# Channel-first inputs, norms on VectorE and combinations on GpSimd in a Strassen-like first stage

## The chip, the cores and the metric

One core of a Trainium2 chip runs one launch. The metric is the device time of that launch in microseconds (us). Engines: TensorE (PE; its weight loads are PEld), VectorE (DVE), ScalarE (ACT), GpSimd (POOL), and SyncE (SP), which issues most DMAs.

## The reference

A gated encoder layer is applied to two token sets, `x_prompt` (1024 tokens of 1024 channels) and `x_sample` (512 tokens). Cut to what matters:

```python
h = rms_norm(x, pre_w)                       # x * rsqrt(mean(x*x) + eps) * pre_w, per token
cols = jnp.einsum('bsd,dc->bsc', h, w_in)    # one combined projection for all branches
...                                          # mLSTM branch, dilated attention branch, gates
out = jnp.einsum('bsd,de->bse', merged, w_out)
return x + rms_norm(out, post_w)
```

Everything is float32, and the change lies in how `h` is made and laid out for the combined projection.

## The kernel before

A float32 product is made of three passes (`mm3`, L193 to L195): every operand is split into a high part, rounded to the format that PE takes at full rate (`AF.Copy` on ACT), and a low part, the difference (on DVE).

For the prompt, `h` (tokens by channels) is divided into four quarters of 512x512, and the projection is a seven-product scheme on 2x2 blocks (Strassen's, in Winograd's form). The seven combinations of quarters are B11, T2, B21, T3, T1, T4 and B22. Each is needed by channel (channels on the 128 partitions, tokens along the row), because PE sums over the partitions. They are kept in `H[0][m]` (high, `Hh`) and `H[1][m]` (low, `Hl`), each 128 x 4 x 512, `k` counting the four groups of 128 channels.

With x(i, j) the quarter of token block i and channel block j after the norm, T1 is x(1,0) - x(0,0), T3 is x(1,1) - x(1,0), T2 is x(1,1) - T1, T4 is x(0,1) - T2; B11, B21 and B22 are x(0,0), x(0,1) and x(1,1).

`value_group(g)` makes the value and gate columns for g = 0 to 3. Group 0 runs first, while the inputs arrive, in the order m1 (B11), m2 (B21), m7 (T3), m6 (T2), m5 (T1), m4 (T4), m3 (B22); each product is 48 matmuls of 128x322. Its weights `wa` and `wb` are summed on DVE (`sums`, and `s[:, 1]` once more after m6's split), and `split` makes high and low parts into two rotating pairs of buffers `vhi`, `vlo`.

The pieces around the change, before:

- `lead` (L344): per token block of 128, ACT squares a row tile and sums it, POOL makes the reciprocal root (`root`, L253), DVE puts it on a diagonal, and PE multiplies the raw rows by this diagonal, which transposes and scales them at once. That gives B11.
- `norm` (L356): DVE scales the whole rows, 128x1024, in place (L359, L266).
- `put(m, k)` (L368): PE transposes, with sums and differences where the combination needs them (products with the identity or its negative, L377 and L379), ACT makes the high part from the bank, and DVE the low part (L383), or, for B21 and B22, PE subtracts the high part in the bank (L387) and ACT copies the rest.
- These calls stand between the quarters of the products (`with_m1` to `with_m6`), so PE's order interleaves them with matmuls.
- `sub` (L361): DVE makes x(1,0) - x(0,0), and x(1,1) minus that, on rows.
- `short_input` (L719): the sample's rows, normed at the end of the first stage, are transposed by PE at the start of the second stage (`turn_in`, L268).

PE's order is the order of the code (`manual_schedule`). The other engines' orders in this first stage are fixed when the program is built, by a scheduler with its own estimates; each engine then runs its instructions strictly in that order, waiting where an input is missing.

Of the kernel before, what the change touches and what calls it, by code (L numbers as in the profile page):

```python
# [176 lines left out]
class Net:  # L177
# [90 lines left out]
    def turn_in(self, parts, ps, out, k, w=None):  # L268

        nc = self.nc  # L270
        p = ps.tile([P, BLK], F32, name="d")
        for t, x in enumerate(parts):
            nc.tensor.transpose(p[:, t * P:(t + 1) * P], x[:, k * P:(k + 1) * P], self.ident)
        hi, lo = (x[:, k] for x in out)
        if w is None:
            end = nc.scalar.activation(hi, p, AF.Copy)
            nc.vector.tensor_sub(lo, p, hi.bitcast(F32))
        else:
            end = nc.scalar.activation(hi, p, AF.Copy, scale=w)
            nc.vector.scalar_tensor_tensor(lo, p, w, hi.bitcast(F32), op0=OP.mult, op1=OP.subtract)  # L280
        return end
# [48 lines left out]
    def combos(self, ps, H, xt, r, junk, pw, minus, again, diag):  # L330

        nc = self.nc
        part = lambda i, j: [x[:, j * BLK:(j + 1) * BLK] for x in xt[i]]
        a0, b0, a1, b1 = part(0, 0), part(0, 1), part(1, 0), part(1, 1)
        plus, neg = self.ident, minus.bitcast(F32)  # L340
        terms = {B21: [(b0, plus)], B22: [(b1, plus)], T3: [(b1, plus), (a1, neg)],
                 T1: [(a0, plus)], T2: [(b1, plus)], T4: [(b0, plus), (b1, neg)]}

        def lead():  # L344
            ps_ = [ps.tile([P, BLK], F32, name="d") for _ in range(4)]
            for t in range(4):
                nc.vector.tensor_scalar(diag[t], self.ident, self.root(xt[0][t], r[t], junk), None, op0=OP.mult)
                for k in range(4):
                    nc.tensor.matmul(ps_[k][:, t * P:(t + 1) * P], a0[t][:, k * P:(k + 1) * P], diag[t], start=t == 0,
                                     stop=True, skip_group_check=True)  # L350
# [5 lines left out]
        def norm(i, t):  # L356
            if i:
                return self.norm(xt[i][t], r[4 * i + t], junk, pw)
            return nc.vector.scalar_tensor_tensor(xt[i][t], xt[i][t], r[t][:, 2:3], pw, op0=OP.mult, op1=OP.mult)  # L359

        def sub(m):  # L361
            for t in range(4):
                if m == T1:
                    nc.vector.tensor_sub(a0[t], a1[t], a0[t])
                else:
                    nc.vector.tensor_sub(b1[t], b1[t], a0[t])

        def put(m, k):  # L368

            if m == T4 and k == 0:  # L370
                again()
            p = ps.tile([P, BLK], F32, name="d")
            for t in range(4):
                for i, (x, one) in enumerate(terms[m]):
                    of, to = x[t][:, k * P:(k + 1) * P], p[:, t * P:(t + 1) * P]
                    if i == 0 and m not in (B21, B22):
                        nc.tensor.transpose(to, of, one)  # L377
                    else:
                        nc.tensor.matmul(to, of, one, start=t == i == 0, stop=True, skip_group_check=True)  # L379
            hi, lo = H[0][m][:, k], H[1][m][:, k]  # L380
            nc.scalar.activation(hi, p, AF.Copy)
            if m not in (B21, B22):
                self.low = nc.vector.tensor_sub(lo, p, hi.bitcast(F32))  # L383
                return None

            def rest():
                nc.tensor.matmul(p, minus, hi, start=False, stop=True, skip_group_check=True)  # L387
                nc.scalar.activation(lo, p, AF.Copy)
            return rest

        return lead, norm, sub, put
# [11 lines left out]
    def value_group(self, g, T, H, sb, us, co, ps, late=None, begin=None, u3=None, more=None, turn=None):  # L403
# [8 lines left out]
        if g:  # L412
            first, wa, wb, s = place(), *self.value_weights(sb)
            for kh in range(2):
                nc.sync.dma_start(wa[:, kh], self.a["w_vp"][g, 0, kh])
            for kh in range(2):
                nc.sync.dma_start(wb[:, kh], self.a["w_vp"][g, 1, kh])
        else:
            first, wa, wb, s, (lead, norm, sub, put) = begin
# [11 lines left out]
        def product(m, w, turns=(), outer=False):  # L431

            banks = [ps.tile([P, BLK], F32, name="d") for _ in range(4)]
            turns = iter(turns)
            if outer:
                next(turns)
            for i in range(4):
# [5 lines left out]
                next(turns, None)  # L443
# [26 lines left out]
        if g == 0:  # L470
            lead()
            w11, low = split(wa[:, 0], first, 2), []

            def with_m1():
                yield
                with self.tc.issue_after(self.low.ins):
                    for t in range(4):
                        last = norm(0, t)
                yield
                with self.tc.issue_after(last.ins):  # L480
                    for t in range(4):
                        last = norm(1, t)
                yield
                low.append(last.ins)
                rest = [put(B21, 0)]
                yield
                for k in range(1, 4):
                    rest.append(put(B21, k))
                    rest.pop(0)()
                rest.pop(0)()  # L490
                yield

            def with_m2():
                rest = [put(B22, 0), put(B22, 1)]
                yield
                rest += [put(B22, 2), put(B22, 3)]
                rest.pop(0)(), rest.pop(0)()
                yield
                put(T3, 0)
                rest.pop(0)(), rest.pop(0)()  # L500
                put(T3, 1)
                yield
                put(T3, 2), put(T3, 3)
                low.append(self.low.ins)
                yield

            def with_m7():
                put(T1, 0), put(T1, 1)
                yield
                put(T1, 2), put(T1, 3)  # L510
                with self.tc.issue_after(low[1]):
                    sub(T2)
                yield
                put(T2, 0), put(T2, 1)
                yield
                put(T2, 2), put(T2, 3)
                low.append(self.low.ins)
                yield

            def with_m6():  # L520
                for k in range(4):
                    put(T4, k)
                    yield

            m1 = product(B11, w11, with_m1(), True)
# [3 lines left out]
            with self.tc.issue_after(low[0]):  # L529
                self.sums(wa, wb, s)  # L530
            m2 = product(B21, w12, with_m2())
# [4 lines left out]
            with self.tc.issue_after(low[0]):  # L536
                sub(T1)
# [3 lines left out]
            with self.tc.issue_after(low[1]):  # L541
                s2 = split(s[:, 1])
            m6 = product(T2, s2, with_m6())
            with self.tc.issue_after(low[2]):
                nc.vector.tensor_sub(s[:, 1], wa[:, 1], s[:, 1])
            for t in range(4):
                add(u2[t], u2[t], m6[t][:, :VW])
                add(u3[t], u3[t], m6[t][:, :VW])
            yield
# [27 lines left out]
        if g == 0:  # L577
            with self.tc.issue_after(low[2]):
                s1 = split(s[:, 0])
        else:  # L580
            s1 = split(s[:, 0])
        m5 = product(T1, s1)
        if g == 0:
            for t, c in enumerate(held):
# [9 lines left out]
        m4 = product(T4, split(wb[:, 1]))  # L594
        for t in range(4):
# [123 lines left out]
    def short_input(self, ps, xt):  # L719
# [1113 lines left out]
def body(tc, a):  # L1833
# [3 lines left out]
    with ExitStack() as st:  # L1837
# [12 lines left out]
        with ExitStack() as s1:  # L1850
# [4 lines left out]
            with ExitStack() as sv:  # L1855
# [5 lines left out]
                one = us.tile([P, VW], F32, name="u2", bufs=4)[0:1, :P]  # L1861
                diag = [us.tile([P, VW], F32, name="u2b", bufs=4)[:, :P] for _ in range(4)]
                xp = N.pool(s3, "x0", 1, "left"), N.pool(s4, "x1", 1, "right")
                xt = [[xp[i].tile([P, D], F32, name=f"x{i}{t}") for t in range(4)] for i in range(2)]
                minus = H[1][T4][:, 3, :P]
                spare = H[0][T4].bitcast(F32).rearrange("p a c -> p (a c)")
# [250 lines left out]
```

## Time and profile before

| | |
|---|---|
| median of 3 runs | 2289.6 us (2284.14 to 2295.39) |
| profiled execution | 2292.12 us, span 2290.3 us |
| PE busy | 2258.5 us, 99% of the span |
| DVE, ACT, POOL busy | 1465.7, 1102.2, 628.6 us |
| first product of group 0 starts | 13.49 us |
| second stage's first product starts | 978.07 us |

A row of a timeline has start, length, engine, line, operation, `output<-inputs`, shapes, count, and in brackets the idle time of the engine before it and what ended it. A row of a group has the count, then busy time and the mean in ns. A row of busy time by stretches has the stretch, its length, busy time of PE, PEld, DVE, ACT and POOL with their counts, the granted clock, the DMA engines' share and GB/s. Names leave out buffer numbers: `Hh`, `Hl` are the combinations, `x` the input tiles.

### The profile page before, as it was taken

Reading aid. Unit: us, or ns where it says so; the run is one execution under the profiler, and the core shown is the slowest. Engines: PE = TensorE matmul, PEld = TensorE weight load, DVE = VectorE, ACT = ScalarE, POOL = GpSimd, SP = SyncE. Lnnn points to the kernel's source line nnn. Section 1 sums busy time; section 2 is a strip of 40 time slices with the busy share of each in tenths; the row PEclk is TensorE's granted clock in tenths of the full one; section 3 lists DMA queues with packets and bytes.
Section 4 is the critical chain, followed back from the end, with each engine's and each line's share of the span. In section 5 each row is a group of like instructions: output and inputs, shape, how many; then the busy total and the mean of one; then the engine's idle time right before and its main releaser. Section 6 shows DMA issues by size and latency. Waiting matters only on the chain. (4 is left out here: it accounts for less than half of the span.)

```text
span 2290.3 us, 36121 instructions
## 1 busy us (share of the span) xinstructions
PE 2258.5 (99%) x12628; PEld 1975.3 (86%) x12628; DVE 1465.7 (64%) x2851; ACT 1102.2 (48%) x2255; POOL 628.6 (27%) x824
## 2 busy tenths in 40 slices
PE   9999999999999999999999999999999999999998
PEld 8999888888878888879999889988888888888887
DVE  7765577688875564466777756674487744555563
ACT  6332243444443343366667656776544444544422
POOL 2000333333332232136556510001032221421311
PEclk9999999999999999999999999999999999999999
DMA  3552455543222243285674679987687878787673
GB/s 126 161 134 71 173 204 194 195 167 113 101 102 83 83 147 110 91 315 154 219 226 138 199 195 243 249 227 214 181 254 242 254 217 241 201 256 210 216 259 113
DMA packets 251903, 416.71 MB, mean 182 GB/s; under 512 B 24993, under 2 KB 150049, under 8 KB 251722
## 3 DMA queue, kind: packets, MB, share of 16 engines
q1 hardware_dynamic: 248120, 401.82, 56.9%
q10 hardware_dynamic: 3602, 12.59, 1.4%
q8 instruction: 100, 1.64, 0.3%
q14 instruction: 81, 0.66, 0.1%
HBM read 294.34 MB, written 128.37 MB: 185 GB/s over the span
## 5 line engine op out<-in xcount | busy, mean ns | idle before, releaser
L193 PE MATMUL dense<-H,wh 128*128 128x512 f32 x672 | 277.5, 413 | 2.3 <-DVE sw L714 1.9
L195 PE MATMUL dense<-H,wl 128*128 128x512 f32 x672 | 263.8, 393 | 0.0
L194 PE MATMUL dense<-H,wh 128*128 128x512 f32 x672 | 263.0, 391 | 0.0
L195 PE MATMUL d<-Hh,phla 128*128 128x512 f32 x608 | 237.0, 390 | 2.2 <-DVE phla L610 2.2
L193 PE MATMUL d<-Hh,phla 128*128 128x512 f32 x608 | 236.6, 389 | 0.0
L194 PE MATMUL d<-Hl,phla 128*128 128x512 f32 x608 | 236.6, 389 | 0.0
L250 DVE TENSOR_TENSOR wl<-wraw,wh 128x1024 fp32r<-128x1024 f32 (+1 forms) x130 | 163.9, 1262 | 106.7 <-ACT wh L249 105.4
L1475 DVE CUSTOM_DVE_ANT_0 ls<-lg,bias 128x256 f32<-128x256 f32 (+1 forms) x288 | 93.7, 361 | 158.9 <-PE lg L1463 53.9
L249 ACT ACTIVATE wh<-wraw 128x1024 fp32r<-128x1024 f32 (+1 forms) x130 | 137.0, 1054 | 97.1 <-PE dense L194 50.0
L628 POOL TENSOR_TENSOR psum_w<-pw_raw 128x512 f32<-128x512 f32 x38 | 61.4, 1617 | 443.4 <-DVE u L596 216.0
L1479 ACT ACTIVATE ls<-ls,nm 128x256 f32<-128x256 f32 (+1 forms) x288 | 130.0, 453 | 102.9 <-DVE nm L1477 87.8
L195 PE MATMUL d<-Hh,phlb 128*128 128x512 f32 x456 | 177.4, 389 | 0.0
L193 PE MATMUL d<-Hh,phlb 128*128 128x512 f32 x456 | 177.4, 389 | 0.0
L194 PE MATMUL d<-Hl,phlb 128*128 128x512 f32 x456 | 177.4, 389 | 0.0
L195 PEld LDWEIGHTS dense<-H,wl 128*128 128x128 f32 x672 | 126.2, 188 | 28.7
L193 PEld LDWEIGHTS dense<-H,wh 128*128 128x128 f32 x672 | 126.6, 188 | 20.4 <-issue 2.3
L194 PEld LDWEIGHTS dense<-H,wh 128*128 128x128 f32 x672 | 127.0, 189 | 17.5
L194 PE MATMUL d<-vlo,Hh 128*128 128x322 f32 x448 | 139.9, 312 | 1.9 <-DVE vlo L427 1.9
L193 PE MATMUL d<-vhi,Hh 128*128 128x322 f32 x448 | 141.0, 315 | 0.3
L195 PE MATMUL d<-vhi,Hl 128*128 128x322 f32 x448 | 140.3, 313 | 0.4 <-DVE Hl L354 0.2
L195 PEld LDWEIGHTS d<-Hh,phla 128*128 128x128 f32 x608 | 114.1, 188 | 27.3 <-DVE phla L610 3.7
L194 PEld LDWEIGHTS d<-Hl,phla 128*128 128x128 f32 x608 | 114.1, 188 | 23.7
(573 smaller groups left out, 6064.2 us busy)
## 6 DMA issues: line engine op xcount, KB each, us to landing
pw_raw<-w_in SPq DMA_DIRECT2D x76, 512.0 KB
wraw<-w_in SPq DMA_DIRECT2D x76, 512.0 KB
aqk_a<-pwk SPq DMA_DIRECT2D x48, 512.0 KB
aqk_b<-sw SPq DMA_DIRECT2D x48, 256.0 KB
wraw<-w_pm SPq DMA_DIRECT2D x24, 512.0 KB
wraw<-w_out SPq DMA_DIRECT2D x24, 512.0 KB
wraw<-w_v SPq DMA_DIRECT2D x18, 512.0 KB
erep<-erow SPq DMA_DIRECT2D x16, 512.0 KB
```

The lines of the kernel that those rows point to most:

```text
L193: nc.tensor.matmul(out, lh, rh, start=start, stop=False)
L194: nc.tensor.matmul(out, lh, rl, start=False, stop=False)
L195: nc.tensor.matmul(out, ll, rh, start=False, stop=stop)
L249: self.splits = (nc.scalar.activation(hi[:, :n], raw[:, :n], AF.Copy), nc.vector.tensor_sub(lo[:, :n], raw[:, :n], hi[:, :n].bitcast(F32)))
L250: nc.vector.tensor_sub(lo[:, :n], raw[:, :n], hi[:, :n].bitcast(F32)))
L628: self.nc.gpsimd.tensor_add(s[:, 0], ws[1][:, 0], ws[1][:, 1])
L1475: nc.vector.tensor_tensor_reduce(out=ls[:, hh], in0=ts["lg"][hh], in1=bt[:, hh], scale=1.0, scalar=NEG, op0=OP.add, op1=OP.max, accum_out= ...
L1479: nc.scalar.activation(ls[:, hh], ls[:, hh], AF.Exp, bias=nm[:, hh:hh + 1], accum_out=ot[:, 128 + hh:129 + hh])
```

## The change

The host hands in the inputs a second time, by channel (`x_prompt_t`, `x_sample_t`), beside the rows. The rows are still loaded, into buffers that T4 and T2 will use, for the row scales and for B11, which is made as before. All other quarters come in by channel (`xq`). The scale of a token then has to lie along the row, the same on all partitions: `spread` multiplies a matrix of ones by the diagonals on PE, and ACT copies the result to `R`. `norm` is now one DVE instruction per 128x512 (times the channel's weight, times R). The subtractions for T3, T1, T2 and T4 are on POOL, 128x512 each, and high and low parts are made from these SBUF tiles. PE's products of group 0 then follow each other without small products in between, and four of them run with `k` outermost. For the sample, the same is done before the second stage, with four ones products ahead of gate pair 5.

```diff
+        self.ones = pool.tile([P, P], F32, name="ones")
+        nc.vector.memset(self.ones, 1.0)
...
-    def combos(self, ps, H, xt, r, junk, pw, minus, again, diag):
+    def combos(self, ps, H, xq, rows, r, junk, diag, R):
+        x = lambda i, j, k: xq[i][j][:, k]
+        def spread(i):
+            p = ps.tile([P, BLK], F32, name="d")
+            for t in range(4):
+                nc.tensor.matmul(p[:, t * P:(t + 1) * P], self.ones, diag[i][t], start=t == 0, stop=True, skip_group_check=True)
+            nc.scalar.activation(R[i], p, AF.Copy)
+        def scale(i, t):
+            return nc.vector.tensor_scalar(diag[i][t], self.ident, self.root(rows(i, t), r[4 * i + t], junk), None, op0=OP.mult)
...
+        def norm(i, j, k):
+            nc.vector.scalar_tensor_tensor(x(i, j, k), x(i, j, k), self.prew[:, 4 * j + k:4 * j + k + 1], R[i], op0=OP.mult,
+                                           op1=OP.mult)
+        def put(m, k, z):
             hi, lo = H[0][m][:, k], H[1][m][:, k]
+            nc.scalar.activation(hi, z, AF.Copy)
+            self.low = nc.vector.tensor_sub(lo, z, hi.bitcast(F32))
...
-            m1 = product(B11, w11, with_m1(), True)
+            w11 = split(wa[:, 0], first, 2)
+            m1 = product(B11, w11, True)
+            for t in range(4):
+                scale(1, t)
+            spread(0)
+            for k in range(4):
+                norm(0, 1, k)
+                put(B21, k, x(0, 1, k))
+            spread(1)
             for t in range(4):
                 nc.scalar.activation(u2[t], m1[t][:, :VW], AF.Copy)
             w12 = split(wa[:, 1])
-            m2 = product(B21, w12, with_m2())
+            m2 = product(B21, w12, True)
+            t3, t2 = again(0), again(1)
+            for k in range(4):
+                norm(1, 0, k)
+                norm(1, 1, k)
+                nc.gpsimd.tensor_sub(t3[:, k], x(1, 1, k), x(1, 0, k))
+                put(T3, k, t3[:, k])
+            self.sums(wa, wb, s)
+            w3 = split(wb[:, 0])
...
-            m7 = product(T3, split(wb[:, 0]), with_m7())
+            m7 = product(T3, w3, True)
+            for k in range(4):
+                norm(0, 0, k)
+                nc.gpsimd.tensor_sub(x(0, 0, k), x(1, 0, k), x(0, 0, k))
+                nc.gpsimd.tensor_sub(t2[:, k], x(1, 1, k), x(0, 0, k))
+                put(T2, k, t2[:, k])
+            s2 = split(s[:, 1])
...
+            m6 = product(T2, s2, True)
+            for k in range(4):
+                put(T1, k, x(0, 0, k))
+            nc.vector.tensor_sub(s[:, 1], wa[:, 1], s[:, 1])
...
+            for k in range(4):
+                nc.gpsimd.tensor_sub(x(0, 1, k), x(0, 1, k), t2[:, k])
...
         m5 = product(T1, s1)
         if g == 0:
+            for k in range(4):
+                put(T4, k, x(0, 1, k))
...
         m4 = product(T4, split(wb[:, 1]))
+        if g == 0:
+            for k in range(4):
+                put(B22, k, x(1, 1, k))
...
-    def short_input(self, ps, xt):
+    def short_input(self, xt):
...
-                end = self.turn_in([x[:, q * BLK:(q + 1) * BLK] for x in xt], ps, (hi, lo), k,
-                                   self.prew[:, 4 * q + k:4 * q + k + 1])
+                end = nc.scalar.activation(hi[:, k], xt[q][:, k], AF.Copy)
+                nc.vector.tensor_sub(lo[:, k], xt[q][:, k], hi[:, k].bitcast(F32))
...
+                rows(0)
                 weights(0, 0)
+                rows(1)
+                load(0, 1)
+                weights(0, 1)
+                load(1, 0)
+                load(1, 1)
+                weights(1, 0)
+                load(0, 0)
+                weights(1, 1)
...
+                    if j == 5:
+                        p = ps.tile([P, BLK], F32, name="d")
+                        for t in range(4):
+                            nc.tensor.matmul(p[:, t * P:(t + 1) * P], N.ones, xdiag[t], start=t == 0, stop=True,
+                                             skip_group_check=True)
+                        nc.scalar.activation(xr, p, AF.Copy)
...
+                    if j in (5, 6):
+                        for k in range(4):
+                            x = xt[j - 5][:, k]
+                            nc.vector.scalar_tensor_tensor(x, x, N.prew[:, 4 * j - 20 + k:4 * j - 19 + k], xr, op0=OP.mult,
+                                                           op1=OP.mult)
```

How the orders move. First DVE, before the change, from the low half of m2's weights (first row) to the low half of m7's weights (last row); `vsum` and `vb` are the weight sums, `x_140` to `x_143` the row tiles of the first token block:

```order
L427 TENSOR_TENSOR vlo<-va,vhi 128x1288
L396 TENSOR_TENSOR vsum<-vb 128x1288
L364 TENSOR_TENSOR x_140<-x_144,x_140 128x512
L364 TENSOR_TENSOR x_141<-x_145,x_141 128x512
L364 TENSOR_TENSOR x_142<-x_146,x_142 128x512
L364 TENSOR_TENSOR x_143<-x_147,x_143 128x512
L397 TENSOR_TENSOR vb<-va,vb 128x1288
L398 TENSOR_TENSOR vsum<-vsum,va 128x1288
L535 TENSOR_TENSOR u2b<-u_170,d 128x322
L535 TENSOR_TENSOR u2b<-u_171,d 128x322
L427 TENSOR_TENSOR vlo<-vb,vhi 128x1288
```

Between the two weight splits stand nine instructions. DVE after the change, from the low half of m2's weights on; `x_150`, `x_151`, `x_152` and `x_149` are x(0,1), x(1,0), x(1,1) and x(0,0), and `Hl_107` is the low part of B21, `Hl_111` that of B22:

```order
L387 TENSOR_TENSOR vlo<-va,vhi 128x1288
L343 SCALAR_TENSOR_TENSOR x_150<-x_150,prew,R_153 128x512 x4
L343 SCALAR_TENSOR_TENSOR x_151<-x_151,prew,R_154 128x512 x4
L349 TENSOR_TENSOR Hl_107<-x_150,Hh_100 128x512
L343 SCALAR_TENSOR_TENSOR x_152<-x_152,prew,R_154 128x512 x2
L349 TENSOR_TENSOR Hl_107<-x_150,Hh_100 128x512 x2
L343 SCALAR_TENSOR_TENSOR x_152<-x_152,prew,R_154 128x512 x2
L349 TENSOR_TENSOR Hl_107<-x_150,Hh_100 128x512
L343 SCALAR_TENSOR_TENSOR x_149<-x_149,prew,R_153 128x512 x2
L349 TENSOR_TENSOR Hl_111<-x_152,Hh_104 128x512
```

The norms of x(1,0) and most of x(1,1) stand ahead of B21's low parts, and B22's come long before m3. Further down the same queue, up to the low half of m7's weights (`vlo<-vb,vhi`); `Hl_109` is T1's low part, `Hl_382` T2's:

```order
L349 TENSOR_TENSOR Hl_382<-Hl_384,Hh_380 128x512
L357 TENSOR_TENSOR vb<-va,vb 128x1288
L358 TENSOR_TENSOR vsum<-vsum,va 128x1288
L349 TENSOR_TENSOR Hl_109<-x_149,Hh_383 128x512 x2
L349 TENSOR_TENSOR Hl_382<-Hl_384,Hh_380 128x512 x3
L387 TENSOR_TENSOR vlo<-vb,vhi 128x1288
L387 TENSOR_TENSOR vlo<-vsum,vhi 128x1288
```

The low half of m7's weights now stands behind the low parts of all of T1 and T2, which only m5 and m6 read. On POOL, where group 0 before had only the roots of the row scales, there now stand (T3 into `Hh_381`, T1 into `x_149`, T2 into `Hl_384`, T4 into `x_150`):

```order
L445 TENSOR_TENSOR Hh_381<-x_152,x_151 128x512 x4
L456 TENSOR_TENSOR x_149<-x_151,x_149 128x512 x2
L457 TENSOR_TENSOR Hl_384<-x_152,x_149 128x512
L456 TENSOR_TENSOR x_149<-x_151,x_149 128x512 x2
L457 TENSOR_TENSOR Hl_384<-x_152,x_149 128x512
L470 TENSOR_TENSOR x_150<-x_150,Hl_384 128x512
L457 TENSOR_TENSOR Hl_384<-x_152,x_149 128x512 x2
L470 TENSOR_TENSOR x_150<-x_150,Hl_384 128x512 x3
```

Sixteen subtractions have come to this queue. On ACT, the high half of m7's weights (`vhi<-vb`) stands between high parts of T4 (`Hh_573`), each of which waits for POOL:

```order
L348 ACTIVATE Hh_573<-x_150 128x512
L386 ACTIVATE vhi<-vb 128x1288
L348 ACTIVATE Hh_573<-x_150 128x512
L386 ACTIVATE vhi<-vsum 128x1288
L348 ACTIVATE Hh_573<-x_150 128x512
```

Two of T4's four high parts come ahead of it. PE's order after group 0 is the same as before, but for the 32 transposes of the sample that go and the four ones products that come.

More of the change, by code (lines that the diff above doesn't have):

```diff
@@ L418, in value_group @@
         else:
-            first, wa, wb, s, (lead, norm, sub, put) = begin
+            first, wa, wb, s, (lead, scale, spread, norm, put, x), again = begin
         def split(x, at=None, parts=1):
@@ L1867, in body @@
[L1867 to L1868 removed]
+                u3 = [us.tile([P, VW], F32, name="u3a", bufs=4) for _ in range(4)]
+                diag = [[us.tile([P, w], F32, name=x, bufs=4)[:, :P] for _ in range(4)] for x, w in (("u2b", VW), ("dg", P))]
+                xp = N.pool(s4, "x1", 1, "right"), N.pool(s3, "x0", 1, "left")
+                xq = [[xp[j].tile([P, 4, BLK], F32, name=f"x{i}{j}") for j in range(2)] for i in range(2)]
```

188 lines of the change are left out of this document (39 added, 149 removed).

## The prediction

> **What bounds the kernel now.** I read the page's busy shares first, then the busy time by stretches, then the timeline of the first 92 us engine by engine, because nearly all that the diff touches runs there.
>
> ```profile
> PE 2258.5 (99%) x12628; PEld 1975.3 (86%) x12628; DVE 1465.7 (64%) x2851; ACT 1102.2 (48%) x2255; POOL 628.6 (27%) x824
> 0.00:92.00 92.00, 86.82 (x585) 82.20 (x586) 68.45 (x105) 47.10 (x83) 11.88 (x25) 1.00 0.38 133
> 92.00:960.00 868.00, 863.94 (x4140) 737.80 (x4139) 584.81 (x677) 332.85 (x375) 239.06 (x193) 1.00 0.39 134
> ```
>
> The columns after the length are busy time of PE, PEld, DVE, ACT and POOL, then clock, DMA share and GB/s. TensorE (PE) bounds everything: from 92 to 960 us it is idle for 4 us in 868. A delay of PE's work in the first 92 us therefore stays a delay to the end, and so does a gain. In the first stretch POOL works 12 us of 92, DVE 68.
>
> ```profile
> 13.49 0.41 PE L193 MATMUL d<-vhi,Hh 128*128 128x322 f32 x1
> 14.27 0.42 PE L195 MATMUL d<-vhi,Hl 128*128 128x322 f32 x1 [0.22 <-DVE Hl L354]
> 27.43 0.32 PE L193 MATMUL d<-vhi,Hh 128*128 128x322 f32 x1
> 29.21 1.95 PE L379 MATMUL d<-ident,x 128*128 128x128 f32 x16
> 44.34 0.39 PE L193 MATMUL d<-vhi,Hh 128*128 128x322 f32 x1
> 68.49 0.39 PE L193 MATMUL d<-vhi,Hh 128*128 128x322 f32 x1
> L377 PE MATMUL d<-ident,x 128*128 128x128 f32 x64 | 12.9, 272 | 0.0
> L379 PE MATMUL d<-Hl,x 128*128 128x128 f32 x64 | 11.0, 275 | 0.0
> L379 PE MATMUL d<-ident,x 128*128 128x128 f32 x64 | 8.5, 278 | 0.7 <-DVE x L359 0.7
> L387 PE MATMUL d<-Hh,Hl 128*128 128x512 f32 x8 | 3.4, 461 | 0.5 <-ACT Hh L381 0.5
> ```
>
> These are PE's rows of group 0. Product m1 starts at 13.49, m2 at 27.43, m7 at 44.34, m5 at 68.49. Between 27.43 and 29.21 stand 12 matmuls, 0.148 us each, so a product of 48 takes 7.1. From m1's start to m5's start PE spends 55.0 us, of which four products are 28.4. The other 26.6 are the transposes and combinations of L377 to L387 and waits among them. After m5's start no transposes are left. So the change can win at most 26.6 us here, and the question is whether the inputs of m2, m7 and m6 come as early as PE then could take them.
>
> **What the change costs: the queue of VectorE (DVE).** PE loses the rows above, and DVE its eight norms of 128x1024. PE's order after the change is m1, eight small products with ones, then m2, m7, m6, m5, m4, m3 with nothing between. All B21, T3, T2 and T1 now come from DVE, ScalarE (ACT) and GpSimd (POOL).
>
> ```profile
> 18.49 1.27 ACT L426 ACTIVATE vhi<-va 128x1288 fp32r<-128x1288 f32 x1
> 22.29 1.46 ACT L527 ACTIVATE u<-d 128x322 f32<-128x322 f32 x4
> 16.11 4.86 DVE L359 SCALAR_TENSOR_TENSOR x<-x,xr,Hh 128x1024 f32<-128x1024 f32 x4
> 25.68 1.49 DVE L427 TENSOR_TENSOR vlo<-va,vhi 128x1288 fp32r<-128x1288 f32 x1
> 27.09 1.48 DVE L396 TENSOR_TENSOR vsum<-vb 128x1288 f32<-128x1288 f32 x1
> 28.50 2.48 DVE L364 TENSOR_TENSOR x<-x,x 128x512 f32<-128x512 f32 x4
> 33.73 0.87 DVE L535 TENSOR_TENSOR u2b<-u,d 128x322 f32<-128x322 f32 x2
> ```
>
> Back to back, DVE takes 1.41 for 128x1288 (25.68 to 27.09), 0.61 for 128x512 (4.86 over four of twice the size; 2.48 over four agrees) and 0.41 for 128x322.
>
> Step 1, to the start of DVE's run. The lead (row scales, B11) is the same, so m1 starts at 13.49, its third matmul waits for the first low part until 14.27 as now (0.48 late), and it ends at 13.49 + 0.48 + 7.1, about 21.0. The spread of the norm weights that PE loses at the very start was ahead of no one on this path. ACT then finishes its third copy of m1 (0.36 each) and only then makes the high half of m2's weights (1.27), so DVE begins the low half at 22.3. PE's ones products (16 records at about 0.11) end at 22.8; they are on the path only in so far as R is copied by ACT at 22.6 to 23.7, while DVE is still at the low half. Cost on the path: none beyond DVE's own queue.
>
> Step 2, DVE's queue from there to the low half of m7's weights. The order puts these in a row: low half of m2's weights; 16 norms (x01, x10, x11, x00, with x10 ahead of the first low part of B21); 20 low parts (B21, B22, T3, T1, T2, four each, B22 being needed only by m3); three weight sums; four adds; low half of m7's weights. That is 5 x 1.41 + 36 x 0.61 + 4 x 0.41 = 30.7 us. DVE never gets a gap, so m7 cannot start before 22.3 + 30.7 = 53.0. m2 waits for B21's first low part behind eight norms, 22.3 + 1.41 + 9 x 0.61 = 29.2, later than the 27.43 of now although PE has fewer small products before it. In the kernel before, m7's low half stands 10 instructions behind m2's; now it is 39.
>
> Step 3, POOL. Its 16 subtractions of 128x512 (T3, T1, T2, T4) all fall into that stretch, and ACT's high half of m7's weights stands behind T4's first two.
>
> ```profile
> 559.43 1.29 POOL L628 TENSOR_TENSOR psum_w<-pw_raw 128x512 f32<-128x512 f32 x1 [5.76 <-DVE pwk L678]
> 560.45 1.36 DVE L680 SCALAR_TENSOR_TENSOR pwk<-pwk 128x1024 f32<-128x1024 f32 x1 [1.13 <-ACT pwk L679]
> 560.80 2.17 POOL L629 TENSOR_TENSOR psum_w<-psum_w,pw_raw 128x512 f32<-128x512 f32 x1
> 561.73 2.32 DVE L678 SCALAR_TENSOR_TENSOR pwk<-c,cws,pwk 128x1024 f32<-128x1024 f32 x1
> 562.91 2.29 POOL L631 TENSOR_TENSOR pw_raw<-pw_raw 128x512 f32<-128x512 f32 x1
> 563.97 0.68 DVE L654 TENSOR_TENSOR c<-pu,d 128x512 f32<-128x512 f32 x1
> 564.57 1.72 DVE L678 SCALAR_TENSOR_TENSOR pwk<-c,cws,pwk 128x1024 f32<-128x1024 f32 x1
> L646 POOL TENSOR_TENSOR psum_w<-pw_raw,psum_w 128x512 f32<-128x512 f32 x38 | 49.3, 1297 | 231.8 <-DVE phla L610 231.8
> L610 DVE TENSOR_TENSOR phla<-pw_raw,phla 128x1024 fp32r<-128x1024 f32 x38 | 56.3, 1481 | 1.4 <-ACT phla L609 1.4
> L610 DVE TENSOR_TENSOR phla<-psum_w,phla 128x1024 fp32r<-128x1024 f32 x38 | 46.5, 1223 | 6.4 <-ACT phla L609 6.3
> ```
>
> Here DVE and POOL meet. POOL's L629 ends at 562.97; DVE's L678, begun at 561.73, ends at 564.05, 1.08 later. POOL's L631, begun at 562.91, ends at 565.20, 1.15 after that DVE instruction; the next L678 ends at 566.29, 1.09 after POOL again. They take turns, each waiting out the other. L654 in between, which reads the products' PSUM bank, keeps its 0.68. The old low parts read such a bank (`p`, L383); the new ones read two SBUF tiles, as norms and weight sums do. So I let every subtraction cost DVE its whole 1.29: 16 x 1.29 = 20.6. The other end is no cost at all. A middle value comes from the group means: DVE's low half beside POOL has 1481 ns against 1223 without it, 0.26 a meeting, 4.2 for 16. I take 20.6, since DVE's queue here is full without a gap like the rows at 560 to 566, while the means include instructions that never met.
>
> [...]
>
> Step 4, the sum for group 0. m7 starts at 53.0 + 20.6 = 73.6 and m6 follows without a wait (T2 and its weights are ready by 75), so m5 starts at 73.6 + 14.2 = 87.8 against 68.49: **+19.3 us**. The 26.6 us of removed work are more than eaten by a PE wait of some 34 us ahead of m7 and 6 ahead of m2. From m5 on DVE and ACT do what they did.
>
> **The smaller terms.** Loads: 4.2 MB more come in at the start.
>
> ```profile
> 5.00:10.00 5.00, 5.00 (x17) 3.28 (x16) 2.24 (x5) 4.16 (x8) 2.42 (x7) 1.00 1.02 416
> 10.00:15.00 5.00, 4.67 (x27) 4.21 (x27) 3.31 (x6) 4.74 (x8) 1.29 (x3) 1.00 1.03 413
> 20.00:25.00 5.00, 4.29 (x33) 4.05 (x33) 5.00 (x5) 3.00 (x9) 3.60 (x3) 1.00 0.06 11
> ```
>
> The engines are full at about 400 GB/s and done by 20 us with 6.8 MB. With 11.0 MB they are done at about 31. In SP's order m2's weights are complete after 6.56 MB, 19.5 us; ACT takes them at 21.0. x10 lands by 22, x11 by 25, x00 by 29, the last weights by 31; DVE takes these at 26, 29, 34 or later and 38 or later. So the loads cost nothing, with a cover of 1.5 us on m2's weights and 4 us or more elsewhere.
>
> PE after a long wait:
>
> ```profile
> 7.05 6.33 PE L349 MATMUL d<-u2b,x 128*128 128x128 f32 x32
> L349 PE MATMUL d<-u2b,x x6: 421/421/421, 9.8 to 10.8; 128*128 128x128 f32 x6
> L349 PE MATMUL d<-u2b,x x11: 274/275/421, 11.7 to 13.1; 128*128 128x128 f32 x11
> ```
>
> After the start PE runs slow, 421 ns for what takes 275 later, though the clock column says 1.00; it works from 7.05 and is fast from about 11.9, some 4.8 us. If a 34 us wait brings that back for m7, it costs 4.8 x (1 - 275/421) = 1.7. No long PE wait stands in this trace; the ends are 0 and 3.4 (both waits). I take **+1.7**. [...]
>
> The short input, at 973 us:
>
> ```profile
> 973.13 2.78 PE L273 MATMUL d<-ident,xs 128*128 128x128 f32 x24
> 977.00 1.31 PE L273 MATMUL d<-ident,xs 128*128 128x128 f32 x8 [1.09 <-DVE H L280]
> 978.07 0.48 PE L193 MATMUL dense<-H,wh 128*128 128x512 f32 x1
> 976.20 4.04 DVE L280 SCALAR_TENSOR_TENSOR H<-d,prew,H 128x512 fp32r<-128x512 f32 x6
> 940.00:950.00 10.00, 10.00 (x45) 8.26 (x44) 4.36 (x6) 2.13 (x2) 0.00 (x0) 1.00 0.01 2
> ```
>
> Now 4.94 us lie between the last gate product and the first dense one. Afterwards the first dense matmul still waits for DVE's first low part, which can end at about 976.8, against 978.5 for the first use of it now: -1.7. Four ones products cost PE 8 x 0.11 = 0.9. The eight norms (4.9 us of DVE) lie beside gate products, where DVE is busy 4.4 us of 10; the adds behind them come up to 4.9 later, and PE has other banks to go on with. Together **-0.8**.
>
> Sum: 19.3 + 1.7 - 0.8 = +20.2. The profiled execution (2292.1, span 2290.3) would become 2312; it stands 2.5 above the median of the runs, so the forecast is 2289.6 + 20.2 = **2310**.
>
> **Rivals.** (a) DVE and POOL hardly disturb each other with these short instructions, so the 20.6 vanish; this decides from a meeting cost under 0.1 us. Then m7 starts at 53.0, m5 at 67.2, -1.3, with the other terms -0.4: 2289, no change. Against it: the rows at 560 to 566. It also bounds the gain: even then there is none, because DVE's 30.7 us alone replace PE's 26.6. (b) They meet in part, because POOL finds its turn while DVE waits for ACT or POOL anyway: 4 to 11 of the 20.6, giving 2293 to 2300. For it: DVE must wait at T3's first low part until POOL's first result. (c) More than forecast: the handovers between POOL, ACT and DVE add up along the chain, or group 1's weights, whose buffer is freed only after group 0's last weight sum, come late; sixteen handovers at 0.6 to 1.1 us each give 2320 to 2328.
>
> **How the numbers follow.** Forecast with full turns (2302 to 2320): 0.70. Rival (b): 0.15, (a): 0.10, (c): 0.05. Half a per cent, 11.4 us, is about what a measurement of this kernel can tell. Slower by more: the forecast, (c) and a little of (b), 0.78. Within: 0.20. Faster by more would need DVE's queue to shrink below its own work, 0.02. The range leaves out (a) and (c): 2294 to 2320.
>
> **What would show it.** Right: in the profile after, PE idle for some 6 us before m2 and over 30 before m7, put down to DVE; m7 starting near 74 and m5 near 88; DVE solid from 22 to 74; POOL's subtractions with means near 1.9 us and DVE's 128x512 low parts well over 0.69. Wrong: m7 near 53 with POOL at 1.3 (rival a); a PE wait on a DMA (loads); m1 starting later than 13.5.

## The result, and the profile after

The changed kernel takes 2312.9 us in the median of five runs (2308.77 to 2316.18), the kernel before on the same chip 2291.9 (five runs): ratio 1.0088, interval 1.0066 to 1.0111. The forecast was 2310, in a range of 2294 to 2320. From median to median that is 21.0 us more, where 20.2 were forecast; the kernel before itself now stands 2.3 above the 2289.6 that the forecast started from. The profiled execution took 2312.57 with a span of 2310.8, 20.5 longer than the span before.

The page's busy shares and three stretches of the changed kernel (columns as in the prediction):

```profile
PE 2235.5 (97%) x12416; PEld 1956.0 (85%) x12416; DVE 1488.5 (64%) x2869; ACT 1099.5 (48%) x2249; POOL 650.9 (28%) x840
0.00:92.00 92.00, 47.80 (x269) 46.27 (x270) 70.73 (x92) 39.87 (x68) 36.10 (x41) 0.76 0.41 152
40.00:66.00 26.00, 0.00 (x0) 0.00 (x0) 26.00 (x20) 7.86 (x15) 20.50 (x14) 0.55 0.00 0
71.00:75.00 4.00, 4.00 (x15) 4.00 (x16) 4.00 (x7) 0.00 (x0) 0.00 (x0) 0.50 0.36 105
```

PE had lost 5 us of the first 92 before; now it loses 44. From 40 to 66 us it does nothing, while DVE is busy every microsecond and POOL for 20.5 of 26. The rows of PE's timeline say which products waited and for what:

```profile
29.79 0.64 PE L195 MATMUL d<-vhi,Hl 128*128 128x322 f32 x1 [4.02 <-DVE Hl L349]
66.34 0.64 PE L193 MATMUL d<-vhi,Hh 128*128 128x322 f32 x1 [26.75 <-ACT vhi L386]
70.86 0.63 PE L194 MATMUL d<-vlo,Hh 128*128 128x322 f32 x1 [3.89 <-DVE vlo L387]
76.66 0.42 PE L194 MATMUL d<-vlo,Hh 128*128 128x322 f32 x1
77.06 0.31 PE L193 MATMUL d<-vhi,Hh 128*128 128x322 f32 x1
87.75 0.31 PE L193 MATMUL d<-vhi,Hh 128*128 128x322 f32 x1
```

m2 gets going at 29.79. The first matmul of m7 runs at 66.34, but its second needs the low half of the weights, and m7 really goes from 70.86. m5 starts at 87.75, against 68.49 before: 19.3 us later. The wait at 66.34 is put down to ACT, and ACT in its turn waited for DVE's weight sum, which stood far back in DVE's queue. That queue is full; ACT's row, and the timelines of POOL and DVE between 41 and 48 us, show with what:

```profile
65.01 1.28 ACT L386 ACTIVATE vhi<-vb 128x1288 fp32r<-128x1288 f32 x1 [0.76 <-DVE vb L357]
42.54 1.74 POOL L457 TENSOR_TENSOR Hl<-x,x 128x512 f32<-128x512 f32 x1
44.20 3.41 POOL L456 TENSOR_TENSOR x<-x,x 128x512 f32<-128x512 f32 x2
41.38 3.45 DVE L343 SCALAR_TENSOR_TENSOR x<-x,prew,R 128x512 f32<-128x512 f32 x2
44.74 1.75 DVE L349 TENSOR_TENSOR Hl<-x,Hh 128x512 fp32r<-128x512 f32 x1
46.41 1.75 DVE L349 TENSOR_TENSOR Hl<-Hh,Hh 128x512 fp32r<-128x512 f32 x1
```

A DVE instruction that takes 0.6 alone has 1.75, a POOL one that takes 1.29 alone has 1.7, and on both engines the starts follow each other at about 1.7 us: one of each in that time. The reading is that neither is slow and each row contains the other engine's turn; the first runs below test it.

### The profile page after: what moved, and what is told of

It is laid out like the page before. It is cut to its first block, busy times and chain, and to the rows that moved or that the text cites. A ratio compares the mean times of both kernels' runs of the same rounds, so it can differ in the third digit from the quotient of the medians.

```text
span 2310.8 us, 35740 instructions
## 1 busy us (share of the span) xinstructions
PE 2235.5 (97%) x12416; PEld 1956.0 (85%) x12416; DVE 1488.5 (64%) x2869; ACT 1099.5 (48%) x2249; POOL 650.9 (28%) x840
## 4 chain that ended last, share of the span: by engine, by line
PE 81%; DMA 6%; DVE 6%; issue 2%; ACT 2%; POOL 1%; SPq 1%; DVEq 0%; POOLq 0%; ACTq 0%
PE d L195 12%; PE d L194 12%; PE d L193 12%; PE dense L193 10%; PE dense L195 10%; PE dense L194 10%; PE o L1422 3%; PE pt L1410 2%; PE lg L1387 2%; PE num L195 1%; PE num L194 1%; PE num L193 1%; PE a L1186 1%; DVE Hl L349 1%; DMA rw<-rw_a 1%
## 5 line engine op out<-in xcount | busy, mean ns | idle before, releaser
L1399 DVE CUSTOM_DVE_ANT_0 ls<-lg,bias 128x256 f32<-128x256 f32 (+1 forms) x288 | 93.7, 362 | 161.4 <-PE lg L1387 59.4
L193 PE MATMUL d<-vhi,Hh 128*128 128x322 f32 x448 | 142.5, 318 | 29.2 <-ACT vhi L386 26.7
L194 PEld LDWEIGHTS dense<-H,wh 128*128 128x128 f32 x672 | 127.7, 190 | 20.2 <-DVE H L651 2.6
```

The source lines that it names most:

```text
L193: nc.tensor.matmul(out, lh, rh, start=start, stop=False)
L194: nc.tensor.matmul(out, lh, rl, start=False, stop=False)
L1399: nc.vector.tensor_tensor_reduce(out=ls[:, hh], in0=ts["lg"][hh], in1=bt[:, hh], scale=1.0, scalar=NEG, op0=OP.add, op1=OP.max, accum_out= ...
```

## Experiments

In the first group of runs one thing of the first stage is changed at a time. To keep the rest fixed, DVE's order is written out in the kernels that touch its instructions, where it is otherwise left to the scheduler; unless a run is about another order, it is the changed kernel's. The runs come from several chips, and each ratio is to the kernel before on the same chip. For each run the place to look at is the same: the second matmul of m7 (70.86 in the changed kernel) and the start of m5 (87.75).

| run | m7 goes | m5 | time | ratio to the kernel before |
|---|---|---|---|---|
| changed kernel | 70.86 | 87.75 | 2312.9 | 1.0088 (1.0066 to 1.0111) |
| 32 columns on POOL | 54.81 | 71.63 | 2294.7 | 1.0008 (0.9996 to 1.0019) |
| 256 columns on POOL | 61.64 | 77.33 | 2302.5 (one run) | |
| all on DVE | 60.72 | 76.94 | 2300.6 | 1.0032 (1.0020 to 1.0045) |
| other order | 44.16 | 74.44 | 2301.6 | 1.0038 (1.0024 to 1.0051) |
| idle products | 71.39 | 85.56 | 2312.1 | 1.0095 (1.0081 to 1.0108) |
| all on DVE, other order | 42.65 | 65.25 | 2295.9 | 1.0026 (1.0015 to 1.0036) |
| the same, norms early | 37.56 | 59.52 | 2291.9 | 1.0006 (0.9997 to 1.0016) |

### Are the turns real? 32 and 256 columns

```diff
-                nc.gpsimd.tensor_sub(t3[:, k], x(1, 1, k), x(1, 0, k))
+                nc.gpsimd.tensor_sub(t3[:, k][:, :32], x(1, 1, k)[:, :32], x(1, 0, k)[:, :32])
... (the same for T1, T2 and T4; in the second run :256)
```

> The sixteen GpSimd subtractions work on 32 of their 512 columns (the other columns of the four combinations are left out); the order on VectorE, ScalarE, GpSimd and TensorE is that of the changed kernel. Theory (turns at the data: VectorE loses about 17 us to GpSimd's subtractions before m7): VectorE's own list from 22.3 us, with 16 norms of 0.67, 20 low parts of 0.61, 3 sums and 2 splits of 1.41 and 4 adds of 0.41, is 31.6 us long, so m7 starts at 54 instead of 70.9 and m5 at 70 to 71 instead of 87.9: about 17 us less, 2296. Rival (the queue's order and its waits set m7, GpSimd is a bystander): m7 stays past 67, 2309 to 2313.

> As the run with 32 columns, with 256 of 512 columns in each GpSimd subtraction (the other columns of the four combinations are left out). Theory (a turn lasts as long as the subtraction, so its price goes by columns): 1.07 us a turn at 512 columns, near 0.07 at 32, so about 0.55 at 256: m7 starts at 62 to 64, between 54.8 and 70.9. Rival (a turn is a fixed fee for an operation that is not tiny): m7 at 68 or later.

Rows of the run with 32 columns: the low half that opens DVE's queue, m7, and one POOL instruction.

```profile
22.74 1.50 DVE L403 TENSOR_TENSOR vlo<-va,vhi 128x1288 fp32r<-128x1288 f32 x1 [2.75 <-ACT vhi L402]
54.81 0.63 PE L194 MATMUL d<-vlo,Hh 128*128 128x322 f32 x1 [3.89 <-DVE vlo L403]
36.18 0.58 POOL L493 TENSOR_TENSOR Hl<-x,x 128x32 f32<-128x32 f32 x1
```

The same two places with 256 columns:

```profile
21.87 1.50 DVE L403 TENSOR_TENSOR vlo<-va,vhi 128x1288 fp32r<-128x1288 f32 x1 [2.75 <-ACT vhi L402]
61.64 0.63 PE L194 MATMUL d<-vlo,Hh 128*128 128x322 f32 x1 [3.89 <-DVE vlo L403]
```

From the opening of the queue to m7 it is 32.07 us with 32 columns, 39.77 with 256 and 48.53 (22.33 to 70.86) with 512. The first 224 columns cost 7.70, the next 256 cost 8.76: for the 16 subtractions 0.0344 and 0.0342 us per column. So the price is a straight line in POOL's columns, as far as three single profiles show. Drawn on to zero columns, DVE's own list is 32.07 - 32 x 0.0343 = 31.0 us, and 16 whole subtractions take 17.6 us from it, 1.10 each. The rival (POOL a bystander) and the fixed fee both fall. The 0.55 a turn that was expected at 256 columns is what was found (8.8 over 16); m7 lies a little below 62 because the queue opened at 21.87 and the list is 31.0, not 31.6. In these two runs POOL takes T4's subtractions in another order than in the changed kernel, but all 16 still end ahead of the low half of m7's weights.

### The subtractions on DVE

```diff
-            nc.gpsimd.tensor_sub(...)    # 16 of them
+            nc.vector.tensor_sub(...)    # 12 ahead of m7's weights, T4's 4 behind
```

> The sixteen subtractions are issued on VectorE, twelve of them ahead of m7's weights in the place where their inputs are ready, the last four behind; the rest of the order is kept. Theory (turns): the twelve add 12 x 0.61 = 7.3 us to VectorE's list of 31.6, and the 17 us of turns are gone: m7 at 61 to 62, m5 at 78 to 79, about 2303. Rival (GpSimd's work costs VectorE little): VectorE's list only gets longer, m7 at 75 to 78, 2318 to 2320.

The group of T3's subtractions on DVE, and m7:

```profile
L481 DVE TENSOR_TENSOR Hh<-x,x 128x512 f32<-128x512 f32 x4 | 2.6, 680 | 0.0
60.72 0.64 PE L194 MATMUL d<-vlo,Hh 128*128 128x322 f32 x1 [3.89 <-DVE vlo L403]
```

DVE does itself what POOL did for it and m7 goes 10.1 us earlier. An operation that costs 0.6 in DVE's queue cost it 1.10 when POOL did it.

### The other order, with POOL as it was

```diff
+                N11(*ks); ... T3 ...; sums for m7; w3 = split(wb[:, 0])   # what m7 needs
+                N00(*ks); ... T2 ...; sum for m6; s2 = split(s[:, 1])     # what m6 needs
+                T1l(*ks); ... B22l(*ks)                                   # low parts needed by m5 and m3
```

> The subtractions stay on GpSimd, whole; only the order on VectorE is another: what m7 needs (the norms of three tile groups, the low parts of B21 and T3, two sums, m7's weights) comes first, then what m6 needs, then the low parts of T1 and B22. Theory of two causes (turns and order): m7's list is 18.9 us and four turns of 1.07, so m7 at 45 to 46; m6's adds 9 us and eight turns, m6 at 62 to 64; m5 at 71 to 73, 2297 to 2300. Rival (only the turns cost, the order doesn't): all twelve turns and norms still stand ahead of m6, m5 at 84 or later, 2309 or more.

```profile
44.16 0.64 PE L194 MATMUL d<-vlo,Hh 128*128 128x322 f32 x1 [0.90 <-DVE vlo L403]
65.50 0.64 PE L194 MATMUL d<-vlo,Hh 128*128 128x322 f32 x1 [10.60 <-DVE vlo L403]
62.89 5.04 DVE L403 TENSOR_TENSOR vlo<-vsum,vhi 128x1288 fp32r<-128x1288 f32 x2
```

m7 goes 26.7 us earlier, and m6 becomes the next to wait, until 65.50. It came later than expected for two reasons. DVE stood idle for 4.3 us in three waits (0.34, 2.16 and 1.84) for T2's high parts, which need POOL's subtractions. And it made m6's weights' low half beside T4's subtractions on POOL: 5.04 for two instructions that take 2.8 alone. m5 gains 13.3 us. So the order that the scheduler gave DVE is a second cause of the loss: 20 low parts and three sums stood ahead of m7's weights; m2 and m7 need eight and two of them.

### The wait's own price: idle products

```diff
+            for _ in range(205):
+                nc.tensor.matmul(banks[0][:, :VW], H[0][B21][:, 0, :P], H[0][B11][:, 0, :VW], start=True, stop=True)
             m7 = ...
```

> The changed kernel with 205 idle products of 322 columns on TensorE between m2 and m7 (0.148 us each, 30 us, into a bank that m7 starts anew), so that TensorE waits about 1 us instead of 26.8 and 3.9. The order of the other engines is the same. Theory (the slow products after the wait are a price of the wait): m7 starts at 70.9 as before, its first 22 products at 0.148 instead of 0.27, m5 2.5 us earlier at 85.3, 2310.3 where the changed kernel has 2312.9. Rival (the slow clock comes from something else, or the time is given back at m5's weights): m5 at 87.5 or later, no change.

PE's rows, and the stretch that had a clock of 0.50 in the changed kernel:

```profile
39.34 30.57 PE L395 MATMUL d<-Hh,Hh 128*128 128x322 f32 x205
71.39 0.42 PE L194 MATMUL d<-vlo,Hh 128*128 128x322 f32 x1 [1.33 <-DVE vlo L387]
70.00:75.00 5.00, 3.67 (x25) 3.62 (x25) 5.00 (x7) 0.06 (x1) 0.00 (x0) 1.00 0.20 68
```

In the changed kernel 22 products after 70.86 follow each other at 0.27 us, then at 0.148, and the granted clock reads 0.50 from 66 to 75. With PE kept busy the clock column reads 1.00 from 40 to 80. From m7 to m5 it is 14.17 us instead of 16.89: the wait's price is 2.7 us, and m5 starts 2.2 earlier. The time did not follow: 1.0095 against 1.0088, on another chip, with overlapping intervals. In the profiles the gain is still there at the first scores of the second stage (1005.35 against 1008.29) and gone at the end (spans of 2310.7 and 2310.8). From those scores to the end single profiles of kernels with the by-channel short input take between 1300.6 and 1305.4 us, so a gain of this size can be lost in one profile. The slow products and the earlier m5 are shown, a gain at the end is not.

### Both at once, and the norms early

```diff
# both: all subtractions on DVE, the order above, and one sum less ahead of m6
+                nc.vector.tensor_sub(wb[:, 0], wa[:, 0], wb[:, 0])      # m7's
+                nc.vector.tensor_sub(s[:, 1], wb[:, 1], wb[:, 0])       # m6's
# norms early, on top of it
             lead()
+            spread(0)
...
+                N01(*ks); B21h(*ks); B21l(*ks)
+                w12 = split(wa[:, 1])
```

> All subtractions on VectorE, and what m7 needs first, then what m6 needs, the rest behind; m6's weight sum is taken as vb minus m7's difference, which needs one operation less ahead of it. Theory (the two causes add): m7's list from 22.1 is 19.3 us, m7 at 41 to 42; m6's 12.7 us more, m6 at 53 to 55, m5 at 61 to 63; T4's low parts and m4's weights stand 19 us behind m6's in the queue, m4 at 73: 22 to 25 us less than the changed kernel, 2288 to 2291, level with the kernel before or 0.2% below it. Rival (VectorE's total work decides, order only shifts it): m4 no earlier than with the subtractions on VectorE alone, where m5 started at 76.9: 2300.

> As the run before it, and the first product with ones is issued ahead of m1 and the low parts of B21 ahead of m2's weights, so that VectorE norms from about 17 us instead of 23.5. Theory (VectorE's queue is the limit until m4, so 4 to 5 us more of it are worth 4 to 5): m2 starts at 22 to 23 instead of 29.8, m7 at 37 to 38, m6 at 49 to 51, m4 at 69: 26 to 29 less than the changed kernel, 2284 to 2287, 0.2 to 0.4% below the kernel before. Rival (the loads, which go on until 30 us, or the weights set it): no gain over the run before it.

Of the first: m7 and m6. Of the second: m7 and m6, and the weights of m4.

```profile
42.65 0.42 PE L194 MATMUL d<-vlo,Hh 128*128 128x322 f32 x1 [1.12 <-DVE vlo L403]
55.84 0.61 PE L193 MATMUL d<-vhi,Hh 128*128 128x322 f32 x1 [4.46 <-DVE u2b L458]
37.56 0.44 PE L194 MATMUL d<-vlo,Hh 128*128 128x322 f32 x1 [1.12 <-DVE vlo L403]
50.76 0.39 PE L193 MATMUL d<-vhi,Hh 128*128 128x322 f32 x1 [4.47 <-DVE u2b L456]
68.62 0.42 PE L194 MATMUL d<-vlo,Hh 128*128 128x322 f32 x1 [1.05 <-DVE vlo L403]
```

In the first stage both came close to what was expected: m5 at 65.25 and at 59.52, the latter 9.0 us ahead of the kernel before. At the end both missed by 5 us: 2295.9 where 2288 to 2291 was expected, and 2291.9 where 2284 to 2287 was. Two causes can be read. The last gate product starts 904.4 us after m5 in the kernel before and 903.6 in the changed one, but 909.9 (59.52 to 969.45) in the early one: of the 9.0 us, 5.5 are used up by the end of the first stage. PE's waits on weights and low parts after m5 account for about 3 of them (4.8 us of waits against 1.9). The longest of these waits, of 2.08 us, comes in a later group:

```profile
138.72 0.42 PE L194 MATMUL d<-vlo,Hh 128*128 128x322 f32 x1 [2.08 <-DVE vlo L403]
```

From 140.37 on, 12 products follow each other at 0.27 us instead of 0.148, which is 1.4 more; with the transposed short input (below) the same place has a wait of 2.39 us and then 11 products at 0.27, from 139.89 on. The remaining 1.2 us were not found. And the second stage gave back more, which is the next question. The gain of the early norms over the run without them, 0.2%, is what was expected of it.

### The short input

Two kernels differ from their partner by the short input alone, and one is the kernel before with only that part of the change.

```diff
-                end = nc.scalar.activation(hi[:, k], xt[q][:, k], AF.Copy)      # by channel
+                end = self.turn_in([x[:, q * BLK:(q + 1) * BLK] for x in xt], ...)  # transposes, as before
```

The changed kernel with the transposes back:

> The changed kernel with the short input of the second stage turned by transposes again, as in the kernel before; the first stage stays as changed. Theory (this part moved nothing, the 1.7 us saved at the passage went to slow products behind the wait): within 1 us of the changed kernel, 2312 to 2314. Rival (as on record, the part is worth 0.8): 2313.7. Second rival (the 1.9 us that the rest of the span grew come from it): 2311.

The kernel before with the by-channel short input:

> The kernel before with only the short input's part of the change (by channel, norms by a product with ones, no transposes at the passage). In the runs so far the passage from the last gate product to the scores of the second stage takes 16.4 to 16.6 us with either form. Theory (the part is worth nothing): ratio to the kernel before 0.9995 to 1.0005. Rival, as on record: 0.8 us less, 0.9996. Rival that the undone part suggests (2308.1 against 2312.9, intervals overlapping): the part costs 4 us, ratio 1.0017.

The norms-early kernel with the transposes back:

> The best order of the first stage (all subtractions on VectorE, what m7 needs first, the first product with ones ahead of m1) with the short input turned by transposes as in the kernel before. Theory (the short input is worth nothing): as the run with the by-channel short input, ratio 1.000 to 1.001 to the kernel before. Rival (the by-channel short input costs 4 us): ratio 0.9985 to 0.999.

They took 2308.1 (1.0069, 1.0052 to 1.0087), 2296.2 (1.0007, 0.9999 to 1.0016) and 2290.6 (0.9985, 0.9975 to 0.9995). The third is the clearest: 0.2% below its partner's 1.0006, the intervals apart, though the two ran on different chips. The second points the same way with an interval that still touches 1, the first overlaps its partner's. So the by-channel short input gains nothing and probably costs something, up to 5 us. Little of it is at the passage from the last gate product to the first scores of the second stage. These are the two, in the kernel before and then in the one with the part alone:

```profile
972.90 0.39 PE L195 MATMUL d<-Hh,phlb 128*128 128x512 f32 x1
989.74 1.95 PE L990 MATMUL a<-Q,K 128*128 128x128 f32 x16
972.91 0.39 PE L195 MATMUL d<-Hh,phlb 128*128 128x512 f32 x1
989.85 1.95 PE L992 MATMUL a<-Q,K 128*128 128x128 f32 x16
```

16.84 and 16.94 us. Over the profiles of all thirteen kernels the passage takes 16.84 with the transposes (four kernels) and 16.9 to 17.1 by channel (nine), once 18.3. Where the profiled executions part is later, between the first rows of these two groups (the kernel before, then the part alone, then the norms-early kernel):

```profile
2015.08 0.39 PE L193 MATMUL dense<-X,K 128*128 128x512 f32 x1
2170.76 0.60 PE L1626 MATMUL tp<-ident,X 128*128 128x128 f32 x4
2014.19 0.39 PE L193 MATMUL dense<-X,K 128*128 128x512 f32 x1
2175.60 0.60 PE L1628 MATMUL tp<-ident,X 128*128 128x128 f32 x4
2009.87 0.39 PE L193 MATMUL dense<-X,K 128*128 128x512 f32 x1
2171.73 0.60 PE L1616 MATMUL tp<-ident,X 128*128 128x128 f32 x4
```

155.7, 161.4 and 161.9 us. PE's waits in that stretch, first in the kernel before, then in the norms-early one:

```profile
PE pt L1486 <- ACT ls L1479: 0.6, 1, 0.6
PE lg L193 <- POOL V0a L1395: 0.6, 1, 0.6
PE pt L1476 <- ACT ls L1469: 1.6, 2, 0.9
PE lg L193 <- POOL V0a L1385: 1.5, 1, 1.5
```

In the whole stretch PE is idle for 7.3 us instead of 2.6, in waits for short handovers of ACT, POOL and DVE, and its busy time is 1.5 longer. But the stretch varies in single profiles whatever the short input: 157.9 in the changed kernel, 160.2 with its transposes back. Over all thirteen it takes 157.9 to 162.6 us by channel (mean 160.6) and 155.7 to 160.2 with the transposes (mean 157.5). The 3.1 between the means would fit a cost of the by-channel form in this stretch; but the ranges overlap, and the kernels differ in the first stage too. What would tie it to the short input stays open.

### A version that beats both

```diff
                 T2h(*ks)
+                for t in ks:
+                    add_held(t)
                 T2l(*ks)
-                for t in ks:
-                    add_held(t)
```

> The run before this one with the four adds that free m2's banks ahead of T2's low parts instead of behind them. m6 waited there for its banks, 4.5 us at its first product. Theory: m6 starts 1 to 1.7 us earlier (49 to 49.7 instead of 50.8), and since VectorE's queue up to m4's weights is as long, 0 to 1 us of it are left at the end. Rival (m6's start carries through): 1.5 us less.

It is the norms-early kernel with the transposed short input and m2's banks freed sooner. m6's first row, and a stretch of PE just before it and one behind it:

```profile
48.27 0.61 PE L193 MATMUL d<-vhi,Hh 128*128 128x322 f32 x1 [2.08 <-DVE u2b L472]
46.00:48.20 2.20, 0.18 (x2) 0.00 (x0) 2.20 (x4) 0.97 (x2) 0.00 (x0) 0.99 0.00 0
48.20:54.00 5.80, 4.90 (x17) 4.53 (x18) 5.80 (x11) 0.93 (x4) 0.00 (x0) 0.50 0.01 3
```

Counted from m7, m6 starts 2.4 us earlier than with the adds behind (10.8 against 13.2), more than the 1 to 1.7 expected; at m5 0.3 of it are left (21.6 us behind m7 against 22.0 in the norms-early kernel). The kernel takes 2288.4, ratio 0.9977 (0.9967 to 0.9986): 0.23% below the kernel before and 1.1% below the changed one. Against the run without the moved adds (0.9985, 0.9975 to 0.9995) it can't be told apart.

## Why the forecast held, term by term

The mechanism was the forecast's: PE waits for m7's weights behind a DVE queue that POOL stretches. The sizes of the terms were off in ways that partly cancelled, so that the sum came closer than its parts.

- **DVE's own list**, 30.7 us: 31.0 by the line through the three column counts. The start at 22.3 was 22.33. One count beside the sum is wrong: with 16 norms, 20 low parts, three sums and four adds between them, m7's low half stands 44 instructions behind m2's, not 39.
- **The turns**, 20.6 us, is the term that was mis-sized: 17.6. The step that failed is "every subtraction costs DVE its whole 1.29". 1.29 is the length of POOL's row where nothing lengthens it (1285 to 1307 ns for the 38 of L646 in the kernel before); what DVE loses is 1.10. The prediction's own rows had a smaller turn already: from 564.05 to 565.20, between the ends of a DVE and a POOL row, it is 1.15. So m7 went at 70.9, not at 73.6.
- **m2's wait** of some 6 us was 2.33 and 4.02; m7's of over 30 was 26.75 and 3.89. As forecast, the first is not on the path.
- **PE after the wait**, +1.7, measured 2.7 with the idle products: the slow spell lasted 6.1 us at 0.27 a product instead of 0.148, where the forecast had 4.8 us at 421 ns instead of 275. With the two products of 14.2 the forecast's terms put m5 at 89.5; it came at 87.75. That step 4, which leaves the slow products out, has 87.8 is luck: turns that were 3.0 too dear stand in for slow products of 2.7.
- **The short input**, -0.8, is another mis-sized term. The transposes' 4.9 us did go, and the first low part is used about as early as forecast, 4.04 us behind the last gate product instead of 5.49. But the dense products now wait for it and then run slow. Their rows in the changed kernel:

```profile
992.65 0.47 PE L193 MATMUL dense<-H,wh 128*128 128x512 f32 x1 [0.87 <-DVE c L589]
995.43 0.80 PE L194 MATMUL dense<-H,wh 128*128 128x512 f32 x1 [2.31 <-DVE H L651]
995.00:1000.00 5.00, 4.57 (x14) 3.70 (x15) 5.00 (x9) 1.96 (x2) 0.00 (x0) 0.66 0.94 345
```

From 995.43 to the first scores it is 12.86 us instead of 11.35, products first at 0.43 instead of 0.23, and this takes the 1.45 back: the passage takes 16.90 us (991.39 to 1008.29) as against 16.84. The prediction charged the slow clock to the long wait alone, not to these waits of 0.87 and 2.31 us, and left out that the transposes had kept PE busy just there (its longest wait was 1.09).

- **The loads** cost nothing, as said: in the changed kernel none of PE's waits in the first 92 us is put down to a transfer.
- **The remainder.** From m5 to the last gate product 0.8 us less than before, from the passage to the end 1.9 more. With +19.3 and the passage's +0.1 that makes the 20.5. The 1.9 is within what single profiles of that last part differ by.

Of the rivals, (a) fell as a mechanism, since turns cost 17.6 us, but its bound was right: with 32 columns, where the turns are nearly gone, the time is level with the kernel before (1.0008), no gain, though m5 came at 71.63 and not at its 67.2. (b) and (c) fell: m7 lay neither 4 to 11 us past 53 nor past 74. The handovers between POOL, ACT and DVE added nothing, since DVE always had other work (26.00 us busy of the 26 from 40 to 66).

Each of the two causes can be priced by itself: no turns, 16.1 us of m5; the subtractions on DVE, 10.8; another order, 13.3; the last two together, 22.5, and with early norms 28.2. The transposes that the change took from PE were worth up to 26.6 us there, and the list that replaces them takes DVE 31.0 us before any turn. The best version gains 0.23% where m5 starts 9.4 us (0.4%) earlier than before.

## What to carry to other kernels

Moving work from a full PE to other engines gains only as far as their queues are shorter; add up the receiving queue up to the instruction that PE waits for, in the order in which it is really issued. Work moved from DVE to GpSimd was not off DVE here: with both queues full, a 128x512 subtraction of two SBUF tiles cost DVE 0.6 when it did it and 1.1 when GpSimd did. Where a scheduler orders the queue, look at how many instructions stand ahead of the one that the bottleneck waits for; writing out that order was worth nearly as much as the whole contention (13.3 and 16.1 us).

## What the runs showed of the hardware

- In the changed kernel DVE and POOL with full queues alternated one instruction at a time: rows of 1.75 and 1.7 us between 41 and 48 us, where such instructions take 0.6 and 1.29 alone. With 32, 256 and 512 columns in POOL's 16 subtractions it was 32.07, 39.77 and 48.53 us from the opening of DVE's queue to m7, which is linear: 2.1 ns per column and instruction (0.0343 us over 16).
- PE's clock fell after the long wait (0.50 from 66 to 75 us in the changed kernel) and after much shorter ones. In the best version it fell after 2.1 us without work: the clock column reads 0.99 in the wait and 0.50 after it. After the 4.47 us wait of the norms-early kernel four products still ran at 0.148 us before the slow ones began. The slow spell lasted 6.1 us (22 products) in the changed kernel, 4.5 us (16) with the subtractions on DVE and 3.2 us (12) in the norms-early kernel. What sets its length was not shown.
- With idle products on PE while m7 waited (39.34 to 71.39, 32 us) the clock column reads 1.00 from 40 to 80, where the changed kernel without them has 0.55 from 40 to 66 and 0.50 from 66 to 75.
